# Two-layer FNet and SSD step: layer 1's gate vector moves out of the scan, to layer 0, the seam and layer 1's output projection

## The chip, the cores and the metric

One core of one Trainium2 chip runs the whole program. The metric is device time in microseconds (us) for one execution, lower is better; a kernel's time is the median over its runs. The profile and the trace come from one profiled execution, whose own time stands beside its span below.

## The reference, cut to what matters

Two groups of tokens (128 context tokens, 256 latent tokens; model width 2048) pass through two layers: layer 0 mixes with a Fourier transform, layer 1 with a bidirectional chunked SSD scan. Each layer has three modulation vectors (shift, scale, gate), computed from a conditioning vector, of which there are two: one for context and one for latent tokens.

```python
for i in range(DEPTH):                       # DEPTH = 2
    mod = jax.nn.silu(cond) @ w_ada[i] + b_ada[i]
    shift = mod[:, None, :D_MODEL]
    scale = mod[:, None, D_MODEL:2 * D_MODEL]
    gate = mod[:, None, 2 * D_MODEL:]
    h = _layer_norm(x) * (1.0 + scale) + shift
    out = mixer_i(h)       # _fourier_mixer or _ssd_mixer: h @ w_in, mixing, @ w_out
    x = _layer_norm(DEEPNORM_ALPHA * x + gate * out, ln_g[i], ln_b[i])
```

A gate is needed only when the mixer's output projection is evacuated; shift and scale of a layer are needed before its input projection. Each of these vectors costs 2048 x 2048 weights (16.8 MB) for two rows of result.

## The kernel before, in words

The 384 tokens are three tiles of 128 partitions (tile 0 context, 1 and 2 latent). Every large weight streams from HBM in units of 512 KB (`raw`, issued on SP's queue, line 66). ScalarE makes the high part of a unit (`whi`, line 59), VectorE the low part (`wlo`, line 60), and TensorE multiplies three times per product (lines 198 to 200 with 384 columns, lines 164 to 166 with 512). The order on each engine is the order in which the Python code issues the work, with buffers deciding what may run ahead.

The stages, with the times that they have in the trace: layer 0's Fourier mixer (290 to 560 us, 64 units), its output projection in column chunks n = 0 to 3 (560 to 852), a seam between the layers (`close0`: LayerNorm, layer 1's modulation, transposes at line 782), the scan (`groups`, eight groups, 890 to 1740), layer 1's output projection (`out_proj` again, 1740 to 2000) and `close1`.

The modulation vectors are computed beside all that, mostly on VectorE:

- `ada_stream` is a generator. A half-vector `vh` has 1024 columns; for each of 16 slices of 128 input rows it loads a 512 KB unit `wada` and adds it, times the conditioning value, to two accumulators (context and latent) with two scalar_tensor_tensor instructions of 128x1024 (line 522; called pairs below). After the 16th slice four matmuls against 32 columns of ones (line 528) sum the partitions, ScalarE copies the result and two DMAs write it to the DRAM scratch `modrow`. One slice is one item.
- `run_ada` is called once for each weight unit: it adds `self.rate` to a debt and takes an item from the generator for each whole one. Layer 0's 96 items (its own gate, then layer 1's shift and scale) go at 0.85 a unit in the Fourier mixer, 0.8 and 0.8 in chunks n = 0 and 1 (16 units each), 0.5 in n = 2 (32 units): 54.4 + 12.8 + 12.8 + 16 = 96, so the last item comes with the last unit of n = 2. `mod1_cols` then loads the rows as `mrows` and transposes them on TensorE (line 575) ahead of the rest of the projection.
- `gate_stream` computes layer 1's gate inside the scan at 0.22 items a unit: 32 units `wg` in the same `raw` slots, 256 scalar_tensor_tensor instructions of 128x256 on `gacc` (line 554), and eight times two matmuls against 128 columns of ones (line 560).

In the scan VectorE also does the convolution (`acc`, line 1061), the masks (`E`, `M`, lines 1129 and 1139) and `xw` (line 1153). TensorE waits for some of these: line 1097 for `xbc`, which ScalarE makes from `acc` (line 1062), and line 1231 for `xw`.

Of the kernel before, what the change touches and what calls it, by code (L numbers as in the profile page):

```python
# [16 lines left out]
D = 2048  # L17
KT = 16
W = 4096
RG = 0.22  # L20
LX = 2
RF, RW = 0.85, (0.8, 0.8, 0.5)
# [8 lines left out]
class Builder:  # L31
# [81 lines left out]
    def setup(self):  # L113
# [3 lines left out]
        nc.vector.memset(self.ones, 1.0)  # L117
        self.mod = [pc.tile([128, KT, 4], F32, tag=f"mod{i}", name=f"mod{i}") for i in range(2)]
# [85 lines left out]
    def layer0(self):  # L204
# [6 lines left out]
        self.adaq = self.ada_stream(pa)  # L211
# [295 lines left out]
    def ada_stream(self, pool):  # L507
# [3 lines left out]
        for v in range(3):  # L511
            for hf in range(2):
                vh = 2 * v + hf
                acc = [pool.tile([128, 1024], F32, tag=f"acc{c}", name=self.nm("acc")) for c in range(2)]
                for c in range(2):
                    nc.gpsimd.memset(acc[c], 0.0)
                    nc.sync.dma_start(acc[c][0:1, :], a["bada1"][vh : vh + 1, :])
                for kt in range(KT):
                    w = pool.tile([128, 1024], F32, tag="rawa", name=self.nm("wada"), bufs=2)
                    nc.sync.dma_start(w, a["wada1"][vh, kt])  # L520
                    for c in range(2):
                        nc.vector.scalar_tensor_tensor(acc[c], w, self.cT[:, kt, c : c + 1], acc[c], op0=ALU.mult, op1=ALU.add)  # L522
                    if kt == KT - 1:
                        ps = self.bank()
                        for c in range(2):
                            for s in range(2):
                                o = 64 * c + 32 * s
                                nc.tensor.matmul(ps[o : o + 32, :], ones, acc[c][:, 512 * s : 512 * s + 512], start=True, stop=True)
                        rows = pool.tile([128, 512], F32, tag="arow", name=self.nm("arow"))
                        nc.scalar.copy(rows, ps)  # L530
                        for c in range(2):
                            o = 1024 * hf
                            nc.gpsimd.dma_start(
                                self.modrow[v][c : c + 1, o : o + 1024].rearrange("c (s n) -> (c s) n", s=2),
                                rows[64 * c : 64 * c + 64 : 32, :],
                            )
                    yield

    def gate_stream(self, pool, wp):

        nc, a = self.nc, self.a
        ones = pool.tile([128, 128], F32, tag="ones", name="ones128")
        nc.gpsimd.memset(ones, 1.0)
        for j in range(8):
            acc = [pool.tile([128, 256], F32, tag=f"gacc{c}", name=self.nm("gacc")) for c in range(2)]
            for c in range(2):
                nc.gpsimd.memset(acc[c], 0.0)
                nc.gpsimd.dma_start(acc[c][0:1, :], a["bgate"][j : j + 1, :])
            for k4 in range(4):
                w = self.rawt("wg")  # L550
                nc.sync.dma_start(w, a["wgate"][j, k4])
                for i in range(4):
                    for c in range(2):
                        nc.vector.scalar_tensor_tensor(  # L554
# [4 lines left out]
            for c in range(2):  # L559
                nc.tensor.matmul(ps[:, 256 * c : 256 * c + 256], ones, acc[c], start=True, stop=True)  # L560
# [852 lines left out]
```

## Time and profile before

| | before |
|---|---|
| median of three runs | 2028.01 us (2024.37 to 2030.5) |
| the profiled execution | 2023.44 us, span 2021.6 us |
| granted TensorE clock, mean | 0.988 |
| busy: TensorE matmul | 1942.5 us (96%) |
| busy: VectorE | 1492.6 us (74%) |
| busy: ScalarE, GpSimd | 882.1 us (44%), 277.9 us (14%) |
| DMA | 388.38 MB, mean 192 GB/s |

In the views PE is TensorE, DVE VectorE, ACT ScalarE, POOL GpSimd, and SP the engine whose queue issues the weight loads. TensorE is busy almost throughout, so time is lost where it stands idle, where its clock is granted at the lower level, and where it runs work that another engine or place could have. A row of the timeline gives start and duration; brackets at its end say how long the engine had been idle and what ended that. Matmuls overlap, so that the distance between two starts, not a duration, is the pace.

### The profile page before, as it was taken

Reading aid. Unit: us, or ns where it says so; the run is one execution under the profiler, and the core shown is the slowest. Engines: PE = TensorE matmul, PEld = TensorE weight load, DVE = VectorE, ACT = ScalarE, POOL = GpSimd, SP = SyncE. Lnnn points to the kernel's source line nnn. Section 1 sums busy time; section 2 is a strip of 40 time slices with the busy share of each in tenths; the row PEclk is TensorE's granted clock in tenths of the full one; section 3 lists DMA queues with packets and bytes.
Section 4 is the critical chain, followed back from the end, with each engine's and each line's share of the span. In section 5 each row is a group of like instructions: output and inputs, shape, how many; then the busy total and the mean of one; then the engine's idle time right before and its main releaser. Section 6 shows DMA issues by size and latency. Waiting matters only on the chain.

```text
span 2021.6 us, 28587 instructions
## 1 busy us (share of the span) xinstructions
PE 1942.5 (96%) x11042; PEld 1754.8 (87%) x11042; DVE 1492.6 (74%) x2091; ACT 882.1 (44%) x1280; POOL 277.9 (14%) x350
## 2 busy tenths in 40 slices
PE   7999999999999998879999999999999999999997
PEld 3888899999987786779989999999999999888885
DVE  4455697779699898599686868797878687662557
ACT  2100142222243233576565655575656466542332
POOL 1000010000001000100132313132222222300001
PEclk9999999999999999989999999999999999999998
DMA  9888756667577787544343444444444433574654
GB/s 356 308 298 291 239 176 210 201 202 229 193 245 270 255 284 250 189 139 147 123 142 126 151 146 137 140 141 146 133 144 133 144 133 108 188 265 137 228 191 146
DMA packets 110960, 388.38 MB, mean 192 GB/s; under 512 B 15604, under 2 KB 16700, under 8 KB 109544
## 3 DMA queue, kind: packets, MB, share of 16 engines
q1 hardware_dynamic: 99816, 357.50, 52.5%
q0 software_dynamic: 9968, 28.45, 4.3%
q8 instruction: 86, 1.41, 0.3%
q10 hardware_dynamic: 1040, 0.60, 0.1%
q14 instruction: 50, 0.41, 0.1%
HBM read 367.55 MB, written 18.94 MB: 191 GB/s over the span
## 4 chain that ended last, share of the span: by engine, by line
PE 70%; DVE 11%; issue 6%; DMA 4%; ACT 4%; POOL 3%; POOLq 0%; ACTq 0%; SPq 0%; DVEq 0%
PE ps L198 11%; PE ps L199 11%; PE ps L200 11%; PE ps L405 9%; PE ps L165 7%; PE ps L164 7%; PE ps L166 7%; DMA wada<-in_wada 2%; DVE wlo L60 2%; DVE acc L1061 2%; PE ps L283 1%; DVE gacc L554 1%; POOL ee L1216 1%; DVE acc L522 1%; PE ps L487 1%
## 5 line engine op out<-in xcount | busy, mean ns | idle before, releaser
L59 ACT CAST whi<-raw 128x1024 fp32r<-128x1024 f32 x384 | 402.2, 1049 | 657.3 <-PE ps L199 348.6
L60 DVE TENSOR_TENSOR wlo<-raw,whi 128x1024 fp32r<-128x1024 f32 x384 | 476.4, 1244 | 213.4 <-ACT whi L59 212.4
L198 PE MATMUL ps<-h,whi 128*128 128x384 f32 x1808 | 618.4, 342 | 1.7 <-ACT h L736 1.7
L200 PE MATMUL ps<-h,wlo 128*128 128x384 f32 x1808 | 607.4, 336 | 2.2 <-DVE wlo L60 2.2
L199 PE MATMUL ps<-h,whi 128*128 128x384 f32 x1808 | 606.2, 335 | 0.5 <-DVE h L739 0.4
L198 PEld LDWEIGHTS ps<-h,whi 128*128 128x128 f32 x1808 | 341.0, 189 | 8.3 <-issue 3.6
L199 PEld LDWEIGHTS ps<-h,whi 128*128 128x128 f32 x1808 | 340.6, 188 | 4.6 <-issue 3.1
L200 PEld LDWEIGHTS ps<-h,wlo 128*128 128x128 f32 x1808 | 340.4, 188 | 4.1 <-DVE wlo L60 4.1
L522 DVE SCALAR_TENSOR_TENSOR acc<-wada,cT,acc 128x1024 f32<-128x1024 f32 x192 | 240.1, 1277 | 28.0 <-DMA wada<-in_wada 22.0
L405 PE MATMUL ps<-hc,wpm 128*128 128x194 f32 x1024 | 179.1, 330 | 0.5 <-DVE hc L328 0.5
L405 PEld LDWEIGHTS ps<-hc,wpm 128*128 128x128 f32 x1024 | 167.3, 190 | 12.6 <-DVE u L418 4.1
L165 PE MATMUL ps<-wlo,h 128*128 128x512 f32 x384 | 150.7, 393 | 1.0 <-DVE wlo L60 0.9
L166 PE MATMUL ps<-whi,h 128*128 128x512 f32 x384 | 150.2, 391 | 0.0
L164 PE MATMUL ps<-whi,h 128*128 128x512 f32 x384 | 149.6, 392 | 0.0
L165 PE MATMUL ps<-wlo,ghl 128*128 128x512 f32 x376 | 148.6, 395 | 0.1
L164 PE MATMUL ps<-whi,ghl 128*128 128x512 f32 x376 | 148.5, 395 | 0.0
L166 PE MATMUL ps<-whi,ghl 128*128 128x512 f32 x376 | 147.9, 393 | 0.0
L554 DVE SCALAR_TENSOR_TENSOR gacc<-wg,cT,gacc 128x256 f32<-128x256 f32 x256 | 126.3, 539 | 27.0 <-DMA wg<-in_wgate 15.7
L1061 DVE SCALAR_TENSOR_TENSOR acc<-cb,c_convw,acc 128x386 f32<-128x386 f32 x192 | 133.0, 693 | 4.4 <-ACT acc L1059 2.4
L388 DVE TENSOR_TENSOR wpm<-raw 128x512 f32<-128x512 f32 x128 | 82.9, 685 | 49.6 <-PE ps L405 47.2
L1138 POOL TENSOR_TENSOR E<-E,E 128x512 f32<-128x512 f32 x48 | 71.2, 1486 | 335.1 <-ACT E L1135 335.1
L165 PEld LDWEIGHTS ps<-wlo,h 128*128 128x128 f32 x384 | 72.6, 189 | 17.8 <-DVE wlo L60 2.7
(287 smaller groups left out, 2227.8 us busy)
## 6 DMA issues: line engine op xcount, KB each, us to landing
raw<-in_wi SPq DMA_DIRECT2D x162, 512.0 KB
wada<-in_wada SPq DMA_DIRECT2D x160, 512.0 KB
raw<-in_wo SPq DMA_DIRECT2D x160, 512.0 KB
raw<-in_wu SPq DMA_DIRECT2D x64, 512.0 KB
raw<-in_wz SPq DMA_DIRECT2D x64, 512.0 KB
wg<-in_wgate SPq DMA_DIRECT2D x32, 512.0 KB
gbuf<-y POOLq DMA_DIRECT2D x32, 192.0 KB, 2.2
gr<-gbuf SPq DMA_DIRECT2D x16, 384.0 KB
```

The lines of the kernel that those rows point to most:

```text
L59: self.nc.scalar.copy(hi, src)
L60: self.nc.vector.tensor_tensor(lo, src, hi.bitcast(F32), op=ALU.subtract)
L164: nc.tensor.matmul(bank, lh[:, c], rh, start=first and i == 0, stop=False)
L165: nc.tensor.matmul(bank, lh[:, c], rl, start=False, stop=False)
L166: nc.tensor.matmul(bank, ll[:, c], rh, start=False, stop=last and i == 1)
L198: nc.tensor.matmul(o, wh[:, c], hh, start=kt == 0, stop=False)
L199: nc.tensor.matmul(o, wh[:, c], hl, start=False, stop=False)
L200: nc.tensor.matmul(o, wl[:, c], hh, start=False, stop=kt == KT - 1)
L405: nc.tensor.matmul(held[j][gi][:, NS * s : NS * s + NS], w[:, o : o + 128], hc[2 * k + i][:, s, :], start=first and i == 0 and s == 0, sto ...
L522: nc.vector.scalar_tensor_tensor(acc[c], w, self.cT[:, kt, c : c + 1], acc[c], op0=ALU.mult, op1=ALU.add)
L554: nc.vector.scalar_tensor_tensor(acc[c], w[:, 256 * i : 256 * i + 256], self.cT[:, 4 * k4 + i, c : c + 1], acc[c], op0=ALU.mult, op1=ALU.add)
L1061: nc.vector.scalar_tensor_tensor(acc, cb[:, k : k + 386], w[:, k : k + 1], acc, op0=ALU.mult, op1=ALU.add)
```

## The change

`gate_stream` is removed. `ada_stream` gets the half-vectors 6 and 7 (layer 1's gate) and takes the half-vectors, weight buffers and accumulators as arguments. In layer 0 it runs through half-vector 6, of which it does only the first 8 slices (`GK`), which makes 104 items, at higher rates. `last_gate` does the other 8 slices in the seam as matmuls against `cT`, adding the accumulators through `pick`. Half-vector 7 runs beside chunks n = 0 and 1 of layer 1's output projection at 0.55 items a unit: 16 items of two instructions in 32 units. `so` gets two buffers and takes in `tri` and `ws`.

```diff
-RG = 0.22
+GK = 8
-RF, RW = 0.85, (0.8, 0.8, 0.5)
+RF, RW, RG = 1.0, (0.7, 0.9, 0.55), 0.55
...
-        self.adaq = self.ada_stream(pa)
+        self.adaq = self.ada_stream(pa, range(7), [("rawa", 2)], ("acc0", "acc1"))
...
+            if vh == 6:
+                self.gacc = acc
+            for kt in range(KT if vh != 6 else KT - GK):
+                tg, nb = wbuf[nw % len(wbuf)]
+                nw += 1
+                w = pool.tile([128, 1024], F32, tag=tg, name=self.nm("wada"), bufs=nb)
+                nc.sync.dma_start(w, a["wada1"][vh, kt])
...
-            self.rate = 0.0 if layer else RW[n]
+            self.rate = RG if layer else RW[n]
...
         next(t0)
+        gate_row = self.last_gate(pool)
...
+            gate_row()
...
+    def last_gate(self, pool):
+
+        nc, a = self.nc, self.a
+        ps = self.bank()
+        rows = [slice(32 * s, 32 * s + 2) for s in range(2)]
+        for kt in range(KT - GK, KT):
+            p, tg = (self.praw, "raw") if kt < KT - GK + 4 else (self.phl, ("whi", "wlo")[kt % 2])
+            w = p.tile([128, 1024], F32, tag=tg, name=self.nm("wg"))
+            nc.sync.dma_start(w, a["wada1"][6, kt])
+            for s in range(2):
+                nc.tensor.matmul(ps[rows[s], :], self.cT[:, kt, :], w[:, 512 * s : 512 * s + 512], start=kt == KT - GK, stop=False)
+        for c in range(2):
+            for s in range(2):
+                nc.tensor.matmul(ps[rows[s], :], self.pick[:, 1 - c : 3 - c], self.gacc[c][:, 512 * s : 512 * s + 512], start=False, stop=c == 1)
+
+        def evac():
+            b = pool.tile([34, 512], F32, tag="tm", name="grow", bufs=1)
+            for s in range(2):
+                nc.scalar.copy(b[rows[s], :], ps[rows[s], :])
+                nc.sync.dma_start(self.modrow[3][:, 512 * s : 512 * s + 512], b[rows[s], :])
+
+        return evac
...
+                bufs = [(f"{x}{k}", 1) for k in range(LX) for x in ("xhi", "xlo")]
+                self.adaq, self.debt = self.ada_stream(pool, (7,), bufs[:3], ("gain0", "gain1")), 0.0
...
-        self.adaq, self.debt, self.rate = self.gate_stream(pool, wp), 0.0, RG
```

TensorE at the end of chunk n = 2, before: `acc` are the last half-vector's accumulators, `mrows` the rows for layer 1's shift and scale.

```order
L165 MATMUL ps_5597<-wlo_6208,ghl_5090 128x512
L166 MATMUL ps_5597<-whi_6207,ghl_5090 128x512
L528 MATMUL ps_6239<-acc_5629,ones_2108 32x512 x2
L528 MATMUL ps_6239<-acc_5630,ones_2108 32x512 x2
L164 MATMUL ps_5598<-whi_6231,ghl_5087 128x512
L165 MATMUL ps_5598<-wlo_6232,ghl_5087 128x512
L166 MATMUL ps_5598<-whi_6231,ghl_5087 128x512
L164 MATMUL ps_5598<-whi_6231,ghl_5090 128x512
L165 MATMUL ps_5598<-wlo_6232,ghl_5090 128x512
L166 MATMUL ps_5598<-whi_6231,ghl_5090 128x512
L575 MATMUL ps_6262<-c_ident,mrows 128x64
L164 MATMUL ps_6332<-whi_6336,h_4558 128x512
```

The same place in the changed kernel (its lines 167 to 169 are the three products, 536 the ones, 556 the transpose), with the ones of half-vector 5 first, from further up:

```order
L169 MATMUL ps_5642<-whi_5850,h_4793 128x512
L536 MATMUL ps_5882<-acc_5349,ones_2081 32x512 x2
L536 MATMUL ps_5882<-acc_5350,ones_2081 32x512 x2
L167 MATMUL ps_5643<-whi_5874,h_4788 128x512
...
L168 MATMUL ps_5643<-wlo_6286,ghl_5125 128x512
L169 MATMUL ps_5643<-whi_6285,ghl_5125 128x512
L556 MATMUL ps_6303<-c_ident,mrows 128x64
L167 MATMUL ps_6373<-whi_6377,h_4606 128x512
```

Between the last ones and the transpose stood six matmuls; now 246 rows stand there.

TensorE in the seam of the changed kernel: `r` is tile 0's residual, `xn` the normalised tile 1, `wg` the slices 8 to 15 of half-vector 6.

```order
L765 MATMUL ps_6680<-c_ident,r_4588 128x128 x4
L792 MATMUL ps_6685<-wg_6686,cT 2x512 x2
L792 MATMUL ps_6685<-wg_6690,cT 2x512 x2
L792 MATMUL ps_6685<-wg_6694,cT 2x512 x2
L792 MATMUL ps_6685<-wg_6698,cT 2x512 x2
L792 MATMUL ps_6685<-wg_6702,cT 2x512 x2
L792 MATMUL ps_6685<-wg_6706,cT 2x512 x2
L792 MATMUL ps_6685<-wg_6710,cT 2x512 x2
L792 MATMUL ps_6685<-wg_6714,cT 2x512 x2
L795 MATMUL ps_6685<-acc_5927,pick 2x512 x2
L795 MATMUL ps_6685<-acc_5928,pick 2x512 x2
L765 MATMUL ps_6840<-c_ident,xn_6809 128x128 x4
```

Before, the transposes of `xn` followed those of `r` directly; now the twenty matmuls of `last_gate` stand between them.

SP's queue at the start of layer 1's output projection in the changed kernel: `raw` is a weight unit, `gr` a piece of the scan's output read back, `wada` and `acc` half-vector 7.

```order
L66 DMA raw_14999<-in_wo 128x1024
L856 DMA gr_15009<-gbuf_95 128x768
L528 DMA wada_14861<-in_wada 128x1024
L528 DMA wada_14933<-in_wada 128x1024
L521 DMA acc_14855<-in_bada 1x1024
L521 DMA acc_14856<-in_bada 1x1024
L528 DMA wada_15005<-in_wada 128x1024
L66 DMA raw_15037<-in_wo 128x1024
```

Before, `raw` and `gr` simply alternated there; now five loads stand ahead of the seventh weight unit.

## Rows read from the trace of the kernel before

**Rows 1.** Waits of TensorE in the scan: us in total, times, longest.
```profile
PE ps L1231 <- DVE xw L1153: 13.6, 7, 3.3
PE ps L1097 <- ACT xbc L1062: 8.1, 5, 3.4
```

**Rows 2.** Timeline of TensorE around the transpose of mrows: start, us, instruction, idle before.
```profile
804.88 0.34 PE L575 MATMUL ps<-c_ident,mrows 64*128 64x64 f32 x1 [6.90 <-DMA mrows<-mrow]
805.14 0.79 PE L164 MATMUL ps<-whi,h 128*128 128x512 f32 x1
...
809.52 0.40 PE L165 MATMUL ps<-wlo,h 128*128 128x512 f32 x1
...
811.36 0.39 PE L164 MATMUL ps<-whi,h 128*128 128x512 f32 x1
811.59 0.39 PE L165 MATMUL ps<-wlo,h 128*128 128x512 f32 x1
```

**Rows 3.** Windows: stretch, length, busy us of each engine, PEclk, DMA share, GB/s.
```profile
805.00:810.00 5.00, 5.00 (x14) 3.88 (x15) 1.63 (x3) 0.21 (x1) 0.21 (x1) 0.56 0.95 303
```

**Rows 4.** Timeline of TensorE at the gate's ones-matmuls in the scan.
```profile
992.01 1.03 PE L560 MATMUL ps<-gacc,ones 128*128 128x256 f32 x4
...
993.05 0.34 PE L199 MATMUL ps<-h,whi 128*128 128x384 f32 x1
```

**Rows 5.** Timeline of TensorE in the scan, rows with an idle time before them.
```profile
940.92 0.45 PE L200 MATMUL ps<-h,wlo 128*128 128x384 f32 x1 [1.70 <-DVE wlo L60]
1031.82 2.07 PE L1231 MATMUL ps<-cbt,xw 128*128 128x128 f32 x8 [2.96 <-DVE xw L1153]
1165.62 0.49 PE L1097 MATMUL ps<-xbc 128*128 128x128 f32 x2 [1.69 <-ACT xbc L1062]
1589.23 0.49 PE L1097 MATMUL ps<-xbc 128*128 128x128 f32 x2 [3.42 <-ACT xbc L1062]
1732.28 2.07 PE L1231 MATMUL ps<-cbt,xw 128*128 128x128 f32 x8 [3.31 <-DVE xw L1153]
```

**Rows 6.** Timeline of VectorE: the gate's instructions ahead of three of these waits.
```profile
1029.90 1.27 DVE L554 SCALAR_TENSOR_TENSOR gacc<-wg,cT,gacc 128x256 f32<-128x256 f32 x3
...
1158.75 2.84 DVE L554 SCALAR_TENSOR_TENSOR gacc<-wg,cT,gacc 128x256 f32<-128x256 f32 x5
...
1581.56 1.01 DVE L554 SCALAR_TENSOR_TENSOR gacc<-wg,cT,gacc 128x256 f32<-128x256 f32 x2 [5.50 <-DMA gacc<-in_bgate]
```

**Rows 7.** Timeline of TensorE at layer 0's ones-matmuls, n = 2.
```profile
795.34 1.06 PE L528 MATMUL ps<-acc,ones 128*32 128x512 f32 x8
796.33 0.50 PE L164 MATMUL ps<-whi,ghl 128*128 128x512 f32 x1
```

**Rows 8.** Timeline of TensorE in the seam.
```profile
851.17 1.91 PE L782 MATMUL ps<-c_ident,r 128*128 128x128 f32 x16
867.25 3.67 PE L782 MATMUL ps<-c_ident,xn 128*128 128x128 f32 x16 [14.17 <-ACT xn L707]
```

**Rows 9.** Windows by stage, columns PE, PEld, DVE, ACT, POOL, PEclk, DMA, GB/s.
```profile
290.00:560.00 270.00, 270.00 (x1568) 266.76 (x1567) 209.90 (x245) 77.60 (x94) 8.96 (x12) 1.00 0.64 209
560.00:645.00 85.00, 85.00 (x395) 71.18 (x394) 80.96 (x97) 36.20 (x56) 6.23 (x10) 1.00 0.78 265
...
890.00:1735.00 845.00, 820.25 (x5087) 792.33 (x5087) 666.10 (x985) 513.20 (x784) 206.30 (x220) 0.99 0.42 137
1735.00:1800.00 65.00, 65.00 (x301) 53.44 (x299) 40.15 (x52) 30.01 (x45) 8.12 (x11) 0.98 0.75 248
```

**Rows 10.** Costliest groups: casts, subtractions, the streams' instructions (busy us, mean ns).
```profile
L59 ACT CAST whi<-raw 128x1024 fp32r<-128x1024 f32 x384 | 402.2, 1049 | 657.3 <-PE ps L199 348.6
L60 DVE TENSOR_TENSOR wlo<-raw,whi 128x1024 fp32r<-128x1024 f32 x384 | 476.4, 1244 | 213.4 <-ACT whi L59 212.4
...
L522 DVE SCALAR_TENSOR_TENSOR acc<-wada,cT,acc 128x1024 f32<-128x1024 f32 x192 | 240.1, 1277 | 28.0 <-DMA wada<-in_wada 22.0
...
L554 DVE SCALAR_TENSOR_TENSOR gacc<-wg,cT,gacc 128x256 f32<-128x256 f32 x256 | 126.3, 539 | 27.0 <-DMA wg<-in_wgate 15.7
```

More of the change, by code (lines that the diff above doesn't have):

```diff
@@ L117, in setup @@
         nc.vector.memset(self.ones, 1.0)
+        self.pick = pc.tile([128, 3], F32, tag="pick", name="pick")
+        nc.vector.memset(self.pick, 0.0)
+        nc.vector.memset(self.pick[:, 1:2], 1.0)
         self.mod = [pc.tile([128, KT, 4], F32, tag=f"mod{i}", name=f"mod{i}") for i in range(2)]
@@ L504, in unfold, with ada_stream @@
             mul(row, o + n + 1, n - 1, back[row])
-    def ada_stream(self, pool):
+    def ada_stream(self, pool, vhs, wbuf, accs):
         nc, a = self.nc, self.a
@@ L510, in ada_stream @@
         nc.vector.memset(ones, 1.0)
[L511 to L545, printed above, removed]
+        nw = 0
+        for vh in vhs:
+            v, hf = vh // 2, vh % 2
+            acc = [pool.tile([128, 1024], F32, tag=g, name=self.nm("acc")) for g in accs]
             for c in range(2):
@@ L547, in gate_stream @@
                 nc.gpsimd.memset(acc[c], 0.0)
[L548 to L552, printed above, removed]
-                    for c in range(2):
-                        nc.vector.scalar_tensor_tensor(
-                            acc[c], w[:, 256 * i : 256 * i + 256], self.cT[:, 4 * k4 + i, c : c + 1], acc[c], op0=ALU.mult, op1=ALU.add
+                nc.sync.dma_start(acc[c][0:1, :], a["bada1"][vh : vh + 1, :])
@@ new lines, in ada_stream @@
+            if vh == 6:
[6 more added lines that the diff above has]
+                for c in range(2):
+                    nc.vector.scalar_tensor_tensor(acc[c], w, self.cT[:, kt, c : c + 1], acc[c], op0=ALU.mult, op1=ALU.add)
+                if kt == KT - 1:
+                    ps = self.bank()
+                    for c in range(2):
+                        for s in range(2):
+                            o = 64 * c + 32 * s
+                            nc.tensor.matmul(ps[o : o + 32, :], ones, acc[c][:, 512 * s : 512 * s + 512], start=True, stop=True)
+                    rows = pool.tile([128, 512], F32, tag="arow", name=self.nm("arow"))
+                    nc.scalar.copy(rows, ps)
+                    for c in range(2):
+                        o = 1024 * hf
+                        nc.gpsimd.dma_start(
+                            self.modrow[v][c : c + 1, o : o + 1024].rearrange("c (s n) -> (c s) n", s=2),
+                            rows[64 * c : 64 * c + 64 : 32, :],
@@ L556, in gate_stream @@
                         )
                 yield
-            ps = self.bank()
-            for c in range(2):
-                nc.tensor.matmul(ps[:, 256 * c : 256 * c + 256], ones, acc[c], start=True, stop=True)
-            row = wp.tile([128, 512], F32, tag="so", name=self.nm("grow"), bufs=1)
-            nc.scalar.copy(row[0:1, :], ps[0:1, :])
-            for c in range(2):
-                nc.gpsimd.dma_start(self.modrow[3][c : c + 1, 256 * j : 256 * j + 256], row[0:1, 256 * c : 256 * c + 256])
@@ L875, in dt_stage @@
         dtb = self.const("dtb", pool, (128, 2))
-        trif = tp.tile([128, 3, 128], F32, tag="y", name="tri", bufs=2)
+        trif = tp.tile([128, 3, 128], F32, tag="so", name="tri", bufs=2)
         nc.sync.dma_start(trif, a["tri"])
@@ L958, in dt_rest @@
         tot = tp.tile([128, 2], F32, tag="tot", name="tot")
-        ws = tp.tile([128, 2, 128], F32, tag="sq", name="ws", bufs=1)
+        ws = tp.tile([128, 2, 128], F32, tag="so", name="ws", bufs=2)
         for k, chunks in enumerate(((0, 0), (1, 2))):
@@ L1079, in groups @@
                 self.pop()
-        self.rate = 0.0
-        for _ in self.adaq:
-            pass
         while pend:
@@ L1237, in f @@
                     )
-                so = wp.tile([128, 512], F32, tag="so", name=self.nm("so"), bufs=1)
+                so = wp.tile([128, 512], F32, tag="so", name=self.nm("so"), bufs=2)
                 nc.scalar.copy(so, p)
```

11 lines of the change are left out of this document (6 added, 5 removed).

## The prediction, made before the run

> **What bounds the kernel now.** TensorE does, nearly everywhere, so I read first the windows by stage [rows 9]: it is busy for the whole of the Fourier mixer and of the first chunk of either output projection, and for 820.25 of 845 us in the scan. What a change elsewhere can give is therefore only what TensorE does or waits for. So the list of its waits comes next, and then its timeline at the three places that the change touches.
>
> The scan has 24.75 us without a matmul. Most of it are the waits for `xw` (13.6 us in 7) and for `xbc` (8.1 us in 5) [rows 1]. Both depend on VectorE, which is busy for 666.10 us there [rows 9], and the timeline of VectorE shows what stands in its queue ahead of them [rows 6]. Outside the scan two waits belong to the change: 6.90 us for `mrows` before the transpose at 804.88 [rows 2], and 14.17 us for `xn` in the seam, which ends at 867.25 [rows 8]. The second is a chain of LayerNorm work on VectorE and ScalarE, which the change leaves as it is; what matters is that TensorE is free there.
>
> **The transpose of mrows.** Half-vector 5 now ends about 12 units into chunk n = 2: 64 items come in the mixer, 11.2 and 14.4 in n = 0 and 1, so 6.4 of the 96 are left, at 0.55 a unit. The order has the last ones 246 rows ahead of the transpose in place of six. At the pace of 0.23 us between two starts [rows 2] that is over 50 us for a copy and two small DMA steps, so the wait of 6.90 us goes. After it TensorE ran on at a lower clock: from 805.14 to 809.52 it started ten matmuls in 4.38 us, where 0.23 each would make 2.3 [rows 2]. The mean granted clock in that window was 0.56 [rows 3], where the mixer had 1.00 [rows 9]: mostly the lower level, 1.2 GHz, after an idle time. Without that, 2.1 us more come back. **-9.0 us.**
>
> **The ones-matmuls in the scan.** From the start at 992.01 to the second product behind it at 993.05 are 1.04 us; the pace there is 0.18 us, so the four passes cost 0.86 [rows 4]. There are eight such places: **-6.9 us**, nothing else in the scan's TensorE order being changed.
>
> **The gate's share of the scan's waits.** Here I choose. The gate's 256 instructions are spread over the scan in blocks; the trace shows blocks ahead of late work: three of them (1.27 us) between `M` and the `xw` that ended the wait at 1031.82, five (2.84 us) ahead of the convolution that ended the one at 1165.62, and at 1581.56 VectorE itself idle for 5.50 us behind a load of the gate's bias, before the wait of 3.42 us at 1589.23 [rows 5, 6]. The `wlo` that was late at 940.92 (1.70) has such a block too [rows 5]. A wait can lose no more than the block before it: 1.27, 1.69, 3.42 and 1.70 at these four. Four others of 1.0 to 1.6 us have blocks ahead in the same way, about 5.3 together; that makes 13.4. Some have none: the longest of the rest, 3.31 us at 1732.28 [rows 5], comes after the gate's last item, and stays. A queue that is shorter lets other work run ahead and some of it will stand where the gate stood, so I take **-12 us**. The bounds are nothing, if all of it is filled by other work, and the whole of the two groups, 21.7 us.
>
> **The seam.** `last_gate` adds twenty matmuls between the transposes of `r` and of `xn`. TensorE is done with the first at 853.1 (851.17 + 1.91) and has nothing to do until 867.25 [rows 8]. No row shows a matmul with two columns of result. The nearest is the ones-matmul: eight passes in four column groups take 0.99 us from its start to that of the next product [rows 7]. Passes over 256 columns take 0.86 for four where one group is used, so over 512 columns 0.43 a pass [rows 4]; eight in turn would take 3.4, and 0.99 means that the four groups ran beside each other, two passes deep. In `last_gate` two groups of 32 columns are used, each with ten matmuls of two passes: beside each other 20 x 0.43 = 8.6 us, in turn 17.2. The first ends at 861.7, inside the idle time, and costs nothing; the second at 870.3, and costs 3. I take the first, **0 us**, since the row has the same two properties, fp32 and 32-column groups. It might also gain up to 2, the clock staying up, as TensorE idles less. If the LayerNorm chain were to become shorter, this cover would be gone, and 8.6 us would show. The Trainium skill, "TensorEngine Tiling (Array Packing)", section Key Properties, says that tiles run matmuls in parallel, and that a change of the tiling mode, not of the tile alone, drains the array. By the first rule the seam costs 0 and the sum stays; if the second struck between the two groups they would run in turn, and the sum would be 3 us less. The trace agrees with the first (0.99 in place of 3.4).
>
> What follows the seam: two copies on ScalarE and two DMA issues on SP at its end, ahead of a few constants for the scan. The work queued behind them is the scan's first weight units, which are needed at 890; I take this within 1 us of nothing, and in the range of this term.
>
> **Layer 0.** The mixer takes 9.6 more items of two instructions of 1277 ns [rows 10], which overlap a little, say 1.2 us each: 23 us of VectorE on 209.90 of 270 [rows 9], which makes 86% busy. Chunk n = 0, where VectorE is at 80.96 of 85 and DMA at 265 GB/s with no idle TensorE [rows 9], says that such a load is carried. Bounds 0 to 4 us (one late `wlo` per half-vector), **+1 us**.
>
> **Layer 1's output projection.** Sixteen items of two instructions, 38 us on VectorE, in chunks n = 0 and 1. In n = 0 these are 8.8 items, 21 us on 40.15 of 65, so 94% [rows 9]: what layer 0's n = 0 carried with no wait. DMA has 4.6 MB more in 65 us: 248 becomes 319 GB/s. On SP's queue two `wada` and two bias loads that wait for buffers and for memsets on GpSimd now stand ahead of the seventh weight unit. What is queued behind is `raw`, then ScalarE's cast, VectorE's `wlo` and TensorE. Bounds: nothing, as in layer 0, and 10 us, if these loads are late by about two units of 4.1 us (65 us for 16) and VectorE can't make it up. Nearer to layer 0's row: **+2 us**. One half-vector's ones-matmul comes here: **+1.0 us** [rows 7].
>
> **The sum**: -9.0 - 6.9 - 12 + 0 + 1 + 2 + 1.0 = -23.9 us, against the profiled execution's 2023.44: 1999.5. That execution is 4.6 us below the median of the runs shown, so for a median I say 2028.01 - 23.9 = **2004**.
>
> **The rivals.**
>
> A. *The scan's waits are only passed on.* With the gate out, `wlo` or the masks stand ahead of `xw` and the convolution. For it: the 3.31 us at 1732.28 have no gate ahead. Against: the idle VectorE at 1581.56 is the gate's alone. The -12 falls away: 2016. Chance 0.18.
>
> B. *The first chunk of layer 1's projection is short of weights*, by its SP queue or DMA: +10 in place of +2, so 2012. For it: DMA's share is 0.75 there already. Against: layer 0's n = 0. Chance 0.13. The Trainium skill, "DMA: Bandwidth & Descriptors", section "Issuing engines are not separate DMA queues", has all DMAs interleave on the same 16 engines; by that rule `wada` takes from `raw` whichever queue it stood in, and the price would be this rival's.
>
> C. *`last_gate` is in the way*: in turn, +3, so 2007; in turn and at the 1.2 GHz level, which doubles 17.2, it would end at 887.5, +20, so 2024. Against: TensorE has been busy until 853.1, so it begins at the full clock. Chance 0.05.
>
> D. *Slower: each unit of the projection's n = 0 and 1 is served in turn.* The single accumulator pair, its three single buffers and the weights' cast and `wlo` would make one chain: load, cast, `wlo`, the pair. It decides from 1.5 us a unit over 16 units (24 us, a cycle of 5.6 instead of 4.1); in full, with 2.1 us for a load (0.52 MB at 248 GB/s), 1.05, 1.24 and 2.4 in turn [rows 9, 10], the cycle is 6.8 us, 2.7 more a unit and 43 in 16: 2045 (2004 - 2 + 43). Against: three `wada` buffers and four `raw` let loads run ahead. Chance 0.06.
>
> E. *The transpose waits as before*, if the rows come late for another reason: 2013. The order speaks against it. Chance 0.02.
>
> My forecast has the other 0.56. Its own range, with the bounds of the scan's term at half, is 1996 to 2011. The range goes up to 2020, which takes in A and B together with some of C, and down to 1990: the two groups of waits whole (-21.7 in place of -12), nothing for layer 0 and the projection (-3). A measurement of this kernel can tell a change of about 0.3%, 6 us, from none, so faster means below 2021.9. Forecast, B and E are all faster, A and C for the most part: 0.86. The same: 0.08, from A with B or C. Slower: 0.06, D.
>
> **What would show it.** No wait before the transpose of `mrows`, and granted clock 1.00 behind it. No line of ones in the scan, and the two groups of waits at 10 us instead of 21.7; at 20 it is A. In the seam the matmuls of `last_gate` from about 853 to 862, the transposes of `xn` still at their wait for ScalarE; if those follow `last_gate` at once, it is C. In layer 1's n = 0 TensorE busy for all but 2 us; waits for `wlo` or `whi` of 10 us say B, of over 24 us D. I am wrong if the scan gives nothing, or if a wait that is not in the list appears in the projection.

## The result, and the profile after

The changed kernel takes 2003.37 us (median of four runs, 2000.38 to 2004.61) against 2027.94 (four runs of the kernel before, one more than ahead of the prediction): a ratio of 0.9878 with a 95% interval of 0.9859 to 0.9897, or 24.6 us less. The forecast was 2004. The profiled execution took 2000.38 us, with a span of 1998.5, which is 23.1 us shorter than the profiled one of before. The sum came out as forecast; its terms did not, and most of this part is on them.

The timeline of TensorE in the changed kernel gives the boundaries of the stages (lines 765 and 201 are the transposes and the scan's first product, 792 and 795 `last_gate`, 167 to 169 the three products of the projection):

```profile
798.96 0.27 PE L556 MATMUL ps<-c_ident,mrows 64*128 64x64 f32 x1
799.16 0.50 PE L167 MATMUL ps<-whi,h 128*128 128x512 f32 x1
...
843.60 1.91 PE L765 MATMUL ps<-c_ident,r 128*128 128x128 f32 x16
845.44 7.04 PE L792 MATMUL ps<-wg,cT 128*2 128x512 f32 x32
852.31 1.89 PE L795 MATMUL ps<-acc,pick 128*2 128x512 f32 x8
859.68 3.57 PE L765 MATMUL ps<-c_ident,xn 128*128 128x128 f32 x16 [5.48 <-ACT xn L689]
...
868.76 0.45 PE L201 MATMUL ps<-h,whi 128*128 128x384 f32 x1 [1.68 <-ACT h L718]
...
1701.42 0.40 PE L167 MATMUL ps<-whi,h 128*128 128x512 f32 x1
...
1975.71 0.39 PE L169 MATMUL ps<-xhi,ghl 128*128 128x512 f32 x1
```

The same boundaries in the kernel before, which the rows ahead of the prediction don't have: the scan's first product, the projection's first and its last.

```profile
876.32 0.44 PE L198 MATMUL ps<-h,whi 128*128 128x384 f32 x1 [1.68 <-ACT h L736]
...
1740.11 0.39 PE L164 MATMUL ps<-whi,h 128*128 128x512 f32 x1
...
2006.24 0.39 PE L166 MATMUL ps<-xhi,ghl 128*128 128x512 f32 x1
```

Subtracting these gives each stage (the projection ends with its last row's start and duration, the tail at the span's end):

| stage | before | after | difference | forecast |
|---|---|---|---|---|
| up to the scan's first product | 876.3 | 868.8 | -7.6 | -8.0 |
| scan | 863.8 | 832.7 | -31.1 | -18.9 |
| layer 1's projection | 266.5 | 274.7 | +8.2 | +3.0 |
| tail after the last matmul | 15.0 | 22.4 | +7.4 | 0 |

So the scan gave 12 us more than forecast, and the projection and the tail took as much back. The transpose and the seam went as worked out: no idle time before the transpose of `mrows`, a granted clock of 1.00 in the 10 us behind it (before, [rows 2] and [rows 3]), and `last_gate` in 8.76 us (845.44 to 854.20, estimate 8.6) inside the idle time before `xn`, of which 5.48 of 14.17 us are left [rows 8].

In the scan the list of TensorE's waits shows what went; columns as in [rows 1]:

```profile
PE ps L1235 <- DVE xw L1157: 5.1, 3, 3.8
PE ps L203 <- DVE wlo L60: 1.0, 2, 0.8
...
PE ps L1101 <- ACT xbc L1069: 0.4, 1, 0.4
```

The waits for `xw` fell from 13.6 to 5.1 us and those for `xbc` from 8.1 to 0.4. One of 3.8 us is left, at the end of the scan, where the 3.31 of before was.

Both traces have the same matmuls in the scan, in the same order, except for the ones-matmuls. Lining them up takes the 31.1 us apart: 19.2 at the 22 places where TensorE idles in one trace or the other, 6.4 at the eight places of the ones-matmuls, 3.9 at other matmuls that began while the granted clock was at the lower of its two levels in either trace, and 1.6 spread over the rest. The scan's idle time falls from 25.4 to 7.4 us.

The windows by stage (columns as in [rows 9]) show VectorE relieved in the scan and loaded in the projection. The first of them takes in the projection's first 33.6 us here, as the scan ends at 1701.42:

```profile
890.00:1735.00 845.00, 837.22 (x5184) 804.91 (x5183) 582.03 (x762) 518.11 (x791) 193.72 (x189) 1.00 0.40 128
1735.00:1800.00 65.00, 62.35 (x266) 50.24 (x266) 58.11 (x69) 25.08 (x32) 0.00 (x0) 0.97 0.87 308
```

Between the stages' own boundaries VectorE is busy for 570.3 us of the scan, before for 681.9, and for 60.7 of the 71.4 us of the projection's chunk n = 0, before for 41.7 of 66.9.

The projection has two stalls that the kernel before does not have, both in chunk n = 0, and lining up the two traces matmul by matmul puts 2.5 us on the first, 4.5 us on the second and 1.2 us on the ones-matmul of half-vector 7. These are TensorE's rows at the two places:

```profile
1727.86 0.50 PE L167 MATMUL ps<-whi,h 128*128 128x512 f32 x1 [0.45 <-ACT h L863]
...
1729.13 0.50 PE L169 MATMUL ps<-whi,h 128*128 128x512 f32 x1 [0.54 <-DVE h L864]
...
1772.79 0.96 PE L167 MATMUL ps<-whi,h 128*128 128x512 f32 x3 [1.63 <-ACT whi L59]
1774.78 0.79 PE L168 MATMUL ps<-wlo,h 128*128 128x512 f32 x1 [1.02 <-DVE wlo L60]
```

Ahead of the first, SP's queue shows the pieces of the scan's output (`gr`) and the weights standing behind `wada`:

```profile
1709.13 0.98 SPq L528 DMA_DIRECT2D wada<-in_wada  x2
1711.65 1.13 SPq L521 DMA_DIRECT2D acc<-in_bada  x2
...
1715.89 0.33 SPq L66 DMA_DIRECT2D raw<-in_wo  x1
1719.80 0.33 SPq L528 DMA_DIRECT2D wada<-in_wada  x1
1720.30 0.54 SPq L856 DMA_DIRECT2D gr<-gbuf  x1
1722.20 0.33 SPq L528 DMA_DIRECT2D wada<-in_wada  x1
1726.35 0.33 SPq L66 DMA_DIRECT2D raw<-in_wo  x1
```

The `wada` at 1719.80 has to wait until VectorE has used one of the three buffers, so the `gr` behind it comes late, and the weight unit at 1726.35 later still. That is not all: the weight unit at 1715.89 was issued ahead of this `wada`, and by the semaphores in the trace it landed only at 1726.14, 10.3 us later, where the one at 1707.62 took 3.9. ScalarE waited for it, and TensorE's first wait is for what ScalarE did next:

```profile
1726.24 1.05 ACT L59 CAST whi<-raw 128x1024 fp32r<-128x1024 f32 x1 [0.67 <-DMA raw<-in_wo]
```

The DMA share was 0.95 to 1.00 from 1710 to 1725. So SP's held queue and the full DMA engines both bear on this stall.

At the second stall ScalarE stood idle and DMA was full:

```profile
1771.60 0.20 ACT L132 ACTIVATE rq<-rv 128x3 f32<-128x3 f32 x1 [7.08 <-DVE rv L131]
1771.71 2.95 ACT L59 CAST whi<-raw 128x1024 fp32r<-128x1024 f32 x3
```

```profile
1760.00:1765.00 5.00, 5.00 (x23) 4.04 (x22) 5.00 (x8) 3.74 (x5) 0.00 (x0) 1.00 1.01 403
1765.00:1770.00 5.00, 5.00 (x24) 4.00 (x23) 2.49 (x3) 0.00 (x0) 0.00 (x0) 1.00 1.00 410
1770.00:1775.00 5.00, 2.35 (x13) 1.70 (x12) 4.34 (x11) 3.06 (x4) 0.00 (x0) 0.94 1.01 406
```

Two causes are possible there: three casts stand behind `rq` in ScalarE's queue (before, they stood ahead of it), or the weights themselves are late. SP's rows ahead of the stall (`r` is the residual, three loads of 1 MB):

```profile
1757.00 1.37 SPq L592 DMA_DIRECT2D r<-x1res  x3
1759.31 4.91 SPq L66 DMA_DIRECT2D raw<-in_wo  x3
```

By their semaphores the three `r` landed at 1764.57, 1767.15 and 1769.67, and the first weight unit behind them at 1770.95, 11.6 us after its issue. So `rq`, behind which the casts began at 1771.71, can have held the first of them for 0.8 us at most. Two experiments test it. The kernel before has the same 3 MB ahead of the same weights, and ScalarE idle for them about as long, without a wait of TensorE:

```profile
1788.93 1.33 SPq L611 DMA_DIRECT2D r<-x1res  x3
```

```profile
1803.30 1.05 ACT L59 CAST whi<-raw 128x1024 fp32r<-128x1024 f32 x1 [7.33 <-DMA raw<-in_wo]
```

There TensorE came to chunk n = 1 at 1806.98, 18.1 us after the first `r` was issued. In the changed kernel it was ready at 1771.2, 14.2 us after.

The tail is no computing: from the last matmul to the last tensor instruction on VectorE and GpSimd both traces agree (11.7 us). It is the longest DRAIN, an instruction at the program's end, on GpSimd's queue. The groups of the program's last line, before and then after, with least, median and longest duration in ns:

```profile
L1406 POOLq DRAIN  x3: 46/99/4164, 2016.7 to 2021.4; - x3
```

```profile
L1408 POOLq DRAIN  x3: 46/99/11592, 1986.1 to 1998.2; - x3
```

The output's last DMA ended 13.4 us behind the last matmul before, and 13.7 after; this DRAIN ended 14.2 us behind it before, and 21.6 after.

### The profile page after: what moved, and what is told of

Same layout as the page of the kernel before. It is cut to its first block, busy times and chain, and to the rows that moved or that the text cites. A ratio compares the mean times of both kernels' runs of the same rounds, so it can differ in the third digit from the quotient of the medians.

```text
span 1998.5 us, 28358 instructions
## 1 busy us (share of the span) xinstructions
PE 1938.2 (97%) x11058; PEld 1745.4 (87%) x11058; DVE 1433.6 (72%) x1886; ACT 878.7 (44%) x1273; POOL 260.2 (13%) x307
## 4 chain that ended last, share of the span: by engine, by line
PE 84%; DVE 5%; DMA 3%; issue 3%; ACT 2%; POOL 2%; SPq 0%; POOLq 0%; ACTq 0%; DVEq 0%
PE ps L201 14%; PE ps L203 14%; PE ps L202 14%; PE ps L408 9%; PE ps L168 8%; PE ps L169 8%; PE ps L167 8%; DMA wada<-in_wada 2%; PE ps L286 1%; PE ps L1205 1%; PE ps L490 1%; PE ps L1193 1%; PE ps L1125 1%; DVE wlo L60 1%; PE ps L1181 1%
## 5 line engine op out<-in xcount | busy, mean ns | idle before, releaser
L60 DVE TENSOR_TENSOR wlo<-raw,whi 128x1024 fp32r<-128x1024 f32 x384 | 481.3, 1258 | 216.1 <-ACT whi L59 214.9
L530 DVE SCALAR_TENSOR_TENSOR acc<-wada,cT,acc 128x1024 f32<-128x1024 f32 x240 | 300.3, 1277 | 29.3 <-DMA wada<-in_wada 23.7
L408 PEld LDWEIGHTS ps<-hc,wpm 128*128 128x128 f32 x1024 | 167.3, 190 | 12.6 <-DVE u L421 4.1
L167 PEld LDWEIGHTS ps<-whi,h 128*128 128x128 f32 x384 | 72.3, 189 | 19.1 <-ACT whi L59 1.7
```

The lines of the kernel that those rows point to most:

```text
L60: self.nc.vector.tensor_tensor(lo, src, hi.bitcast(F32), op=ALU.subtract)
L167: nc.tensor.matmul(bank, lh[:, c], rh, start=first and i == 0, stop=False)
L408: nc.tensor.matmul(held[j][gi][:, NS * s : NS * s + NS], w[:, o : o + 128], hc[2 * k + i][:, s, :], start=first and i == 0 and s == 0, sto ...
```

## The experiments

Stages of the profiled execution of each, in us, as in the table above:

| kernel | scan begins | scan | projection | tail |
|---|---|---|---|---|
| 1, after without half-vector 7 | 871.0 | 838.2 | 265.8 | 22.3 |
| 2, before without the sums on VectorE | 880.3 | 839.6 | 266.0 | 15.0 |
| 3, before without the ones-matmuls | 877.8 | 868.9 | 265.8 | 15.0 |
| 4, before at rate 1.0 in the mixer | 871.4 | 866.6 | 266.2 | 15.0 |
| 5, after with later rates | 875.6 | 832.2 | 274.1 | 22.4 |
| 6, as 1, cleaner | 869.0 | 832.0 | 265.9 | 22.4 |
| 7, after with the old buffers | 870.9 | 832.2 | 275.4 | 22.4 |
| 8, before with one sum in eight | 874.8 | 843.3 | 266.0 | 15.0 |
| 9, after with more DMAs on GpSimd | 873.4 | 833.5 | 274.2 | 14.6 |
| 10, after with early RMS | 871.9 | 832.3 | 276.5 | 22.4 |
| 11, all three | 868.6 | 833.7 | 271.9 | 15.1 |
| 12, and the residual in pieces | 870.0 | 833.1 | 268.7 | 14.8 |

These are single executions. Of the first column only differences of several us mean something: kernels 5, 6, 7 and 10 are the same up to the seam, and begin the scan between 869.0 and 875.6. The other three columns repeat within 2 us where the code is the same, except that the scan of before took 863.8 us there and 866.6 in kernel 4, with the same idle time (25.4 and 25.0 us) and more time at the lower clock (17.1 and 23.9).

**1. The projection without half-vector 7.**

```diff
-                self.adaq, self.debt = self.ada_stream(pool, (7,), bufs[:3], ("gain0", "gain1")), 0.0
+                self.adaq, self.debt = iter(()), 0.0
...
-                nc.sync.dma_start(self.modrow[3][:, 512 * s : 512 * s + 512], b[rows[s], :])
+                for o in (0, 1024):
+                    nc.sync.dma_start(self.modrow[3][:, o + 512 * s : o + 512 * s + 512], b[rows[s], :])
```

> The changed kernel without half-vector 7 in layer 1's output projection (its half of the gate is filled with a copy of the other half, so that part of the result is left out). In the changed kernel's trace the projection is 8.1 us longer than before, against 3 predicted. Theory (half-vector 7's loads and instructions delay the reading of the scan's output, the residual and wlo): about 8 us less than the changed kernel, so 1995 us, with the projection's first two chunks as long as before the change. Rival (the projection is late because something else moved, such as the buffers or the end of the scan): 2002 us or more.

Measured: 2003.47 us, ratio 0.9878 (0.9866 to 0.9891), so nothing gained. But the projection is at 265.8 us, as before the change. What it gave, the scan took, 5.5 us, and the part up to the scan 2.3, which is within what that column scatters. SP's queue has two more small issues at the end of the seam, and behind them a weight unit now stands ahead of the scan's constants and waits until 887.59; the first constant came at 888.06, in the changed kernel at 881.40:

```profile
882.73 1.15 SPq L802 DMA_DIRECT2D mrow<-grow  x4
887.59 0.36 SPq L66 DMA_DIRECT2D raw<-in_wi  x1
888.06 0.37 SPq L94 DMA_DIRECT2D c_dtb<-in_dtb  x1
```

The edit had a cost of its own, so the median can't test the theory; the stage can.

**6. The same without that cost** (one DMA on GpSimd's queue fills the row).

```diff
+                f = pool.tile([128, 1024], F32, tag="gain0", name="fill")
+                nc.gpsimd.memset(f, 0.0)
+                nc.gpsimd.dma_start(self.modrow[3][:, 1024:2048], f[0:2, :])
...
```

> As the first experiment (no half-vector 7 in the projection, whose half of the gate is zeros, so that it is left out), but without its two more issues on SP's queue in the seam, behind which a weight unit came 5 us later and the scan's first group took 7.6 us more: one small DMA on GpSimd's queue at the start of the projection fills the row in their place. Theory: the projection gives back its 8 us and the scan stays as in the changed kernel: 1995 us. Rival (the scan's first group varies by itself): 2000 us or more.

Measured: 1994.81 us, ratio 0.9836 (0.9822 to 0.985), the scan at 832.0 and the projection at 265.9. Half-vector 7 costs the projection 8.8 us (274.7 in the changed kernel), the theory's 8.

**2. The scan without the sums on VectorE.**

```diff
-                for i in range(4):
-                    for c in range(2):
-                        nc.vector.scalar_tensor_tensor(
-                            acc[c], w[:, 256 * i : 256 * i + 256], self.cT[:, 4 * k4 + i, c : c + 1], acc[c], op0=ALU.mult, op1=ALU.add
-                        )
```

> The kernel before with the gate's 256 accumulating VectorE instructions left out (the gate is then only its bias); the loads of its weights, the ones-matmuls, copies and DMAs stay. Theory (the scan's waits come from VectorE's queue, and the lower clock from those waits): the waits for xw and xbc fall from 21.7 to about 6 us and some 24 us go, so 2004 us. Rival 1 (the scan loses to the gate's loads and the raw slots they hold): 2020 us or more. Rival 2, my prediction's size: 12 us, so 2016 us.

Measured: 2001.82 us, ratio 0.9874 (0.9861 to 0.9887). The scan is 24.2 us shorter; loads and ones-matmuls, which stayed, are no part of that. The two groups of waits are at the changed kernel's level:

```profile
PE ps L1226 <- DVE xw L1148: 5.4, 3, 3.8
...
PE ps L1092 <- ACT xbc L1057: 0.4, 1, 0.4
```

Lined up with the kernel before, 19.4 of the 24.2 us are at the places with a wait and 3.8 at other matmuls at the lower clock. The theory holds, with its size; my 12 us does not.

**8. One sum in eight.**

```diff
-                for i in range(4):
-                    for c in range(2):
+                for i in range(1):
+                    for c in range(1):
```

> The kernel before with one in eight of the gate's accumulating instructions (the rest of the sum is left out): VectorE still waits for each load of weights and bias in its order, but spends about 13 us on them in place of 103. Theory (VectorE's busy time is what delays xw and the convolution): about as without them all, 2002 to 2006 us. Rival (VectorE standing at late loads is what delays them): 2015 us or more.

Measured: 2003.17 us, ratio 0.9883 (0.9867 to 0.99); the scan is 20.5 us shorter than before. So it is the time that the instructions take on VectorE: with an eighth of them, still in order behind their loads, only 3.7 us of the 24.2 remain.

**3. The scan without the ones-matmuls.**

```diff
-            ps = self.bank()
-            for c in range(2):
-                nc.tensor.matmul(ps[:, 256 * c : 256 * c + 256], ones, acc[c], start=True, stop=True)
...
-            nc.scalar.copy(row[0:1, :], ps[0:1, :])
+            for c in range(2):
+                nc.scalar.copy(row[0:1, 256 * c : 256 * c + 256], acc[c][0:1, :])
```

> The kernel before without the eight pairs of ones-matmuls in the scan (the sum over partitions is left out; the copy takes one partition of the accumulators). Theory: 6.9 us less, as predicted, so 2021 us. Rival (the pairs stand in waits that TensorE has anyway, so that taking them out only lengthens these): 0 to 3 us less, 2025 us or more.

Measured: 2024.64 us, ratio 0.9984 (0.9975 to 0.9994): 3.2 us less, with an interval of 1.2 to 5.1, below the theory's 6.9 and at the rival's edge. The profiled execution took 2029.34 us, 4.7 above the median, and its scan is not shorter at all. Lined up with the kernel before, 6.4 us are gone at the eight places of the ones-matmuls, and 4.4 have come in waits and 7.6 at the lower clock:

```profile
PE ps L1229 <- DVE xw L1151: 12.7, 6, 3.8
PE ps L1095 <- ACT xbc L1060: 8.5, 4, 3.7
PE ps L200 <- DVE wlo L60: 8.3, 6, 4.3
```

Those for `wlo` are at 8.3 us in six waits. In the kernel before they were:

```profile
PE ps L200 <- DVE wlo L60: 2.2, 4, 1.7
```

So the ones-matmuls' own time went, and the median says that about half of it came back elsewhere. That it comes back because TensorE then reaches its waits for VectorE sooner fits the rows, but is not shown: one execution can't tell what the edit lengthened from what varies anyway. With the sums gone, all of it shows: the changed kernel's scan is 6.9 us shorter than experiment 2's (832.7 against 839.6), 6.4 of it at these eight places.

**4. The move of half-vector 5 by itself**, in the kernel before.

```diff
-RF, RW = 0.85, (0.8, 0.8, 0.5)
+RF, RW = 1.0, (0.8, 0.8, 0.5)
```

> The kernel before with the rate of the modulation stream raised from 0.85 to 1.0 in the Fourier mixer and nothing else, so that half-vector 5 ends 13 units into chunk n = 2. Theory: the wait of 6.9 us for mrows and the 2.1 us of lower clock behind it go, and up to 1 us comes back in layer 0: 8 to 9 us less, so 2019 to 2020 us. Rival (the wait is for something that is late anyway, or the mixer pays for the 9.6 more items): 0 to 4 us less, 2024 us or more.

Measured: 2022.3 us, ratio 0.9975 (0.9963 to 0.9987), 5.1 us less with an interval of 2.6 to 7.5. The wait before `mrows` is gone, as the theory has it, and the scan begins 4.9 us earlier, where the wait and the pace behind it are worth 9, so about 4 us were lost in layer 0 in place of the expected 1. Theory and rival each had half. The traces taken together say how much is the fuller layer 0's: from the mixer's first product on `hc` (46.00 in the kernel before) to the transpose, the wait for `mrows` taken off, the four kernels with the old rates take 752.0 to 754.8 us, this one 756.1, and the nine with the changed layer 0 take 753.2 to 759.8. The means are 752.8 and 755.5 for the four and the nine, so the cost is about 2.7 us, with a scatter as large.

**7. The old buffers for `so`, `tri` and `ws`** in the changed kernel.

```diff
-        trif = tp.tile([128, 3, 128], F32, tag="so", name="tri", bufs=2)
+        trif = tp.tile([128, 3, 128], F32, tag="y", name="tri", bufs=2)
...
-        ws = tp.tile([128, 2, 128], F32, tag="so", name="ws", bufs=2)
+        ws = tp.tile([128, 2, 128], F32, tag="sq", name="ws", bufs=1)
...
-                so = wp.tile([128, 512], F32, tag="so", name=self.nm("so"), bufs=2)
+                so = wp.tile([128, 512], F32, tag="so", name=self.nm("so"), bufs=1)
```

> The changed kernel with so, tri and ws buffered as before (one so buffer, tri and ws in their old tiles). Theory (the scan's gain is the gate's alone): no change within 2 us, 2003 us. Rival (the second so buffer gives part of the 31 us by which the scan is shorter): 2007 us or more.

Measured: 2004.47 us, ratio 0.9887 (0.9873 to 0.99), the scan at 832.2: the second buffer gives nothing.

**5. Half-vector 7 later.**

```diff
-            self.rate = RG if layer else RW[n]
+            self.rate = (0.25, 0.85)[n] if layer else RW[n]
```

> The changed kernel with half-vector 7 at 0.25 items a unit in chunk n = 0 and 0.85 in n = 1, in place of 0.55 in both. Theory (the projection's loss is two stalls in n = 0: SP's queue held by wada loads that wait for their buffers, with the scan's output and weights behind them, 2.5 us; and the residual's three loads of 1 MB late beside wada at the end of n = 0, 4.5 us): both mostly go, 5 to 7 us less, so 1997 us. Rival (the loss follows the loads wherever they are): the stalls come in n = 1 and the time stays at 2003 us.

Measured: 2004.04 us, ratio 0.9886 (0.9873 to 0.99), so nothing gained. The first stall is gone, as theory had it, and the second is 6.8 us in place of 4.5:

```profile
1778.74 1.65 PE L167 MATMUL ps<-whi,h 128*128 128x512 f32 x3 [4.00 <-ACT whi L59]
```

At the first place the DMA share is 0.98 to 1.01 from 1715 to 1730 here too, without a stall, so full engines alone don't make one; the thinner `wada` relieve SP's queue and the engines together, and no run takes the two apart. The second stall does not shrink with the rate in n = 0.

**10. The RMS early**, so that `rq` is out of ScalarE's way at the end of n = 0 (`arr1_chunk` calls `mid` after the ninth unit).

```diff
-            self.arr1_chunk(banks, lhs, w[n], 16)
+            early = []
+            self.arr1_chunk(banks, lhs, w[n], 16, mid=(lambda: early.append(rms())) if rms is not None and n == 0 else None)
...
```

> The changed kernel with the RMS of the scan's output (the matmul, the VectorE steps and ScalarE's rq) computed after the ninth unit of chunk n = 0 in layer 1's projection, in place of after the last. In ScalarE's order of the changed kernel rq stands ahead of the first casts of chunk n = 1 (before the change three casts stood ahead of it), and it waits until VectorE has scaled the residual, which is late. Theory (the 4.5 us at the end of n = 0 are these casts behind rq): 4 to 5 us less than the changed kernel, 1999 us, no wait of TensorE for whi and wlo there. Rival (the late residual itself or the DMA share holds TensorE): the time stays at 2003 us.

Measured: 2005.07 us, ratio 0.9892 (0.9874 to 0.9911), the projection 1.8 us longer (it scatters by about 1 between executions). The theory falls. ScalarE has no `rq` there now, and idles for as long, until a weight unit lands, while DMA is full:

```profile
1775.26 1.05 ACT L59 CAST whi<-raw 128x1024 fp32r<-128x1024 f32 x1 [7.74 <-DMA raw<-in_wo]
...
1776.36 1.05 PE L167 MATMUL ps<-whi,h 128*128 128x512 f32 x3 [2.87 <-ACT whi L59]
```

```profile
1765.00:1770.00 5.00, 5.00 (x22) 3.86 (x22) 5.00 (x7) 1.12 (x2) 0.00 (x0) 1.00 1.01 416
```

**9. More DMAs on GpSimd's queue**, for the tail. Counted in the traces, GpSimd issues 151 DMAs in the kernel before and 121 in the changed one, which dropped the gate's small ones.

```diff
-            tc.keep_in_program_order(nc.gpsimd.dma_start(t, a["ln"][o : o + 1, 1024 * hf : 1024 * hf + 1024].to_broadcast([128, 1024])))
+            q = 512 if layer else 256
+            for j in range(0, 1024, q):
+                tc.keep_in_program_order(nc.gpsimd.dma_start(t[:, j : j + q], a["ln"][o : o + 1, 1024 * hf + j : 1024 * hf + j + q].to_broadcast([128, q])))
```

> The changed kernel with the eight loads of the LayerNorm gains on GpSimd's queue split (in four in layer 0, in two in layer 1), the same bytes in 16 more DMAs: 137 in place of 121. At the end of the program GpSimd's DRAIN took 4.16 us in five kernels with 151 DMAs on its queue, and 11.43, 11.51 and 11.59 us in those with 119, 120 and 121: 80 ns for each DMA. Theory (the count starts again after 128): DRAIN takes about 4.16 - 14 x 0.08 = 3.0 us, the span ends with the output's DMAs, 7 us earlier, 1996 us. Rival 1 (DRAIN depends on something else that the change removed): it stays at 11.6 us, 2003 us. Rival 2 (80 ns for each DMA without a new start): 12.9 us, 2004.5 us.

Measured: 1997.18 us, ratio 0.985 (0.9835 to 0.9866), 6.2 us below the changed kernel's median, with a tail of 14.6 us. DRAIN is what the count says, 3.02 us for the expected 3.0:

```profile
L1410 POOLq DRAIN  x3: 46/103/3017, 1991.1 to 1995.5; - x3
```

**11. Experiments 5, 9 and 10 together.**

> Both of these with the later rates (0.25 and 0.85 items a unit) of the earlier experiment, where the first stall of 2.5 us was gone and the second had grown from 4.5 to 6.8 us. Theory: 7 us from the end of the program, 4.5 from rq and 2.5 from SP's queue: 2003.4 - 14 = 1989 us. Rival (the stalls move on in the projection): 1996 us.

Measured: 1994.81 us, ratio 0.9836 (0.9819 to 0.9853). That is the rival's 1996 rather than the theory's 1989. The tail is short and the first stall is down to 0.7 us; the second is still 3.6.

**12. The residual in pieces**, on top of 11.

```diff
+        def residual(n, m):
+            cs = slice(512 * n, 512 * (n + m))
+            for t in range(3):
+                tc.keep_in_program_order(nc.sync.dma_start(r[t][:, cs], xres[t][:, cs]))
+                nc.vector.tensor_scalar(r[t][:, cs], r[t][:, cs], ALPHA, None, op0=ALU.mult)
...
```

> The kernel of the last experiment, with the residual of layer 1's output projection loaded and scaled by columns: 0.75 MB before the evacuation of n = 0, as much for n = 1 and the rest for n = 2 and 3, in place of 3 MB at the end of n = 0. With the RMS early, ScalarE's first casts of n = 1 still began only after an idle time of 7.7 us, ended by a weight unit, and DMA was at 400 GB/s and a share of 1.0 for 15 us there. Theory (the 3 MB stand ahead of the weights on full DMA engines): the 3.5 us that the last experiment still lost at that place fall below 1, about 1991 us. Rival (VectorE, which scales and evacuates there, holds up wlo): the loss stays and the time is 1994 us or more.

Measured: 1988.18 us, ratio 0.9815 (0.9799 to 0.983), the fastest here: 38.6 us below the 2026.78 of before in the same comparison, and its interval lies below the changed kernel's. At the end of n = 0 there is no wait, and DMA has room:

```profile
1765.00:1770.00 5.00, 5.00 (x22) 3.74 (x21) 5.00 (x8) 2.10 (x2) 0.00 (x0) 1.00 0.85 311
```

Of the 3.6 us at that place and just behind it, 0.8 is left. The edit also cuts VectorE's scaling of the residual in pieces, so by itself it doesn't rule out the rival; the landings do more: the first weight unit behind the residual landed 6.8 us after its issue, in place of 11.6 in the changed kernel, and that stretch lies between SP and the DMA engines. So the second stall was the residual's 3 MB ahead of the weights, on DMA engines that half-vector 7's loads had filled.

## Why the prediction was right, and where it was not

The time was right to 0.6 us, and the sign and size of the total with it; that it was so close is luck, as the steps show:

- **The transpose of mrows** (-9.0) and **layer 0** (+1): together -7.6 up to the scan. The wait of 6.90 us and the low pace behind it are gone. Of the cost, 1.0 us shows ahead of the transpose (798.96, where 804.88 - 6.90 would be 797.98). That is one execution against one: over all profiled ones the fuller layer 0 costs 2.7 us (experiment 4), and the scan begins 6.3 us earlier on average (877.3 in four kernels, 871.0 in nine). So +1 was too small by about 2 us.
- **The seam** (0): right in mechanism and number. The two column groups ran beside each other, 8.76 us for an estimate of 8.6, and the transposes of `xn` still waited for ScalarE. Rival C did not come.
- **The ones-matmuls** (-6.9): nearly the right size, 6.4 us at the eight places, in the changed kernel and in experiment 3. But by themselves they give only about half (experiment 3), so the term holds in full only beside the next one.
- **The scan's waits** (-12): the step that failed. I held that a wait can lose no more than the block of gate instructions directly ahead of it. Experiment 2 measured -24.2. In it and in the change also waits went that had no block ahead, such as 1.21 us at 1270.70 in the kernel before. So what delays `xw` and `xbc` is the time that the gate takes of VectorE as a whole (experiments 2 and 8), not the last entry in its queue; I read it as a backlog made earlier, which no run traces back entry by entry. The scan's idle time fell by 18.0 us, 16.2 of them in the two groups (21.7 to 5.5). With the slow matmuls right behind the waits that makes the 19.2 above, and the lower clock elsewhere gave 3.9 more. The term and its bound, the two groups whole, left that clock out.
- **Layer 1's projection** (+2, and +1.0 for the ones): mis-sized; it measured +8.2, 1.2 of it the ones-matmul. Rival B, which I gave 0.13, came with 7.0 of its price of 10. Layer 0's n = 0 was the wrong row to go by: it carries the same load on VectorE, but not the reading of the scan's output through the same SP queue, a place that cost 2.5 us (experiment 5 removes it). The order showed three `wada` ahead of the seventh weight unit, where I counted two. The residual's 3 MB at the end I had not counted: they cost nothing before, but with `wada` beside them DMA stood at 400 GB/s for 15 us and TensorE came to chunk n = 1 about 4 us sooner after them, which made 4.5 (experiment 12, after experiment 10 had ruled out `rq`). My own sign of being wrong came too: the waits for `h` at 1727.86 and 1729.13 are not in the list. The rule of the Trainium skill that I set beside rival B ("DMA: Bandwidth & Descriptors", section "Issuing engines are not separate DMA queues") agrees with the second of these two costs: share 1.0 at 410 GB/s, and the weights late.
- **The tail** (nothing in the sum): +7.4, a step that I had not seen: the change removes DMAs from GpSimd's queue, and the DRAIN there gets longer. Experiment 9 shows it.

So two errors, 12.2 us too little in the scan and 12.6 us too little cost behind it, cancelled, and nothing in the prediction said that they would. The range, and the statement of the total, survive; the terms don't.

## What to carry to other kernels

What an engine's work costs the one that waits for it is not the block ahead of the late instruction: take the work out as a whole on the chip, once, and measure the stage. When work moves into another stage, count what that stage already has at its worst moment on the same queue and the same DMA engines (here the 3 MB of residual), not its mean. And compare stage by stage even where the total fits: 38.6 us were to be had here, and the total alone gave no reason to look.

## What the runs showed of the hardware that was not expected

At the program's end the DRAIN on GpSimd's queue took a time that went with how many DMAs GpSimd had issued in the whole program: 11.43, 11.51 and 11.59 us for 119, 120 and 121, which is 80 ns for each, though the last of them was issued over 130 us earlier; 3.02 for 137 and 4.16 for 151, which is 82 ns for each again, from a lower start. Somewhere between 121 and 137 the time falls back; the runs don't say where. In each trace the DRAIN begins as GpSimd's last tensor instruction does, so that 1.6 us of it may be that. The kernel before had the larger count and the shorter end, so removing thirty small DMAs made the program 7.4 us longer there.

Twenty fp32 matmuls with two columns of result, in two column groups, took 8.76 us. Two passes each make twenty passes in a group, so 0.44 us for a pass of 512 columns, where the passes with 128 columns of result in [rows 4] give 0.43: the narrower result makes a pass no shorter, and the two groups ran beside each other.
